# Dilated window attention in a three-layer kernel: scores in four accumulators, value transposes one projection later, and sums spread by products on all rows

## The chip, the core and the metric

The kernel runs on one core of a Trainium2 chip. Its engines work side by side, each in the order of its own queue: TensorE (PE; its weight loads are listed as PEld), VectorE (DVE), ScalarE (ACT), GpSimd (POOL) and SyncE (SP), which here only issues DMAs. The metric is the device time of the whole program in microseconds, as the median of several runs. All data are fp32.

## What is computed

Two layers of a first block (gated linear attention beside latent attention) and one layer of a second block (three dilated window attentions, a spatial gating unit, cross attention to a memory, and a feed-forward part). The change touches the dilated attention alone. For 512 tokens and three groups of four heads of width 64 it computes, cut down:

```python
for gi, (win, dil) in enumerate(((128, 1), (512, 4), (2048, 16))):
    # query t sees keys t, t-dil, ..., t-win
    s = q @ k.T * 64 ** -0.5 - slope * distance      # masked outside the window
    mx = max(s); e = exp(s - mx); den = sum(e)
    outs.append(e @ v / den); lses.append(mx + log(den))
alpha = softmax(stack(lses), axis=0)                  # over the three groups
y_attn = sum(alpha[..., None] * outs, axis=0)
```

## The kernel before

`mixer` is the second block's first stage. All its projections are matrix products in three parts: weights and activations are split into a high and a low fp32r part, and `mm3` (L202 to L204) adds high by high, high by low and low by high. A projection of 128 output columns is 24 such products on 512 token columns. Weights come in units through `Weights.ahead`: SyncE loads halves of a unit into one of three raw buffers (L90), ScalarE casts the high part (L93), VectorE subtracts for the low part (L94). One unit is fetched ahead of the one in use.

Accumulators lie in pools: two of kind `z` (projections), two `tr` (transposes), three `s`, one `o`. Who asks for a buffer waits until its last reader is done. The order in which each engine meets the work is that of the code, adjusted by a scheduler that moves an instruction up where it reckons that the one ahead would wait.

For each group g, the code projects q and k (four projections, j = 0 to 3), then v. The projections run on activations that are not yet normalised; `r_cols` (L319, L322, L216) turns the sum of squares, which GpSimd adds up, into r, one number for each token, and `r_bcast` (L331, L333) spreads r over all rows as R. `place` multiplies a finished projection by R on VectorE (L1024, L1027). In group 0 `r_cols` stands after the projection j = 0 and `r_bcast` after j = 1.

`scores(g, t, qk)` handles 128 queries (block t of four). Two heads lie in each 128 rows of q and k, so a product (L1038) uses 64 rows, and `par` says which half; each half has an accumulator of its own, of kind `s`. VectorE then scales and adds the bias (L1047) and takes the maximum over the keys (L1049). Group 0 sees 256 keys from its second block on, the dilated groups 128. Group 0 calls `scores` for its four blocks after its v; a dilated group calls it for two blocks after each of the two v projections. An fp32 product outside `mm3` is two instructions in the trace, a transpose (L211) one.

`turn_values` transposes the projected v of a dilated group by blocks into `tr` accumulators, and ScalarE copies them out (L1057).

`maxima` transposes the 12 x 4 maxima for each group to four rows by 512 tokens, joins them there by VectorE (L1268, L1270), and transposes the result back as bias of the exponentials. `turn` and `values` then run over eight parts, with the projections of the gating unit as filling (`fill()` issues half a projection at a time). The sums of the exponentials are in `den`.

`spread` transposes the sums to four rows, adds them (L1293, L1295), takes the reciprocal (L1296), spreads it by a product of four rows with `sel` (L1300) over the 64 rows of each head, and multiplies (L1302). The spatial gating that follows normalises by L1196 to L1199 and mixes by products at L1206.

Of the kernel before, what the change touches and what calls it, by code (L numbers as in the profile page):

```python
# [10 lines left out]
F32 = mybir.dt.float32  # L11
F32R = mybir.dt.float32r
I32 = mybir.dt.int32
AF = mybir.ActivationFunctionType
ALU = mybir.AluOpType
# [138 lines left out]
class K:  # L154
# [836 lines left out]
    def mixer(self, scope):  # L991
# [38 lines left out]
        def scores(g, t, qk):  # L1030
            wide = g == 0 and t > 0
            n = 256 if wide else P
            kc = slice((t - 1) * P, (t + 1) * P) if wide else tsl[t]
            pss = [self.psum("s", (P, 2, 256)) for _ in range(2)]
            for i in range(2):
                for par in range(2):
                    b = slice(64 * par, 64 * par + 64)
                    nc.tensor.matmul(pss[par][:, i, 0:n], qk[b, i, tsl[t]], qk[b, 2 + i, kc],  # L1038
                                     start=True, stop=True)
            for par in range(2):  # L1040
                if g == 0:
                    S = S1[t // 2][:, t % 2, par::2, 256 - n:256]
                    bias = tb1[:, par::2, 256 - n:256]
                else:
                    S = S23[g - 1][:, t, par::2, :]
                    bias = tb23[g - 1][:, par::2, :]
                nc.vector.scalar_tensor_tensor(S, pss[par][:, :, 0:n], 0.125, bias,  # L1047
                                               ALU.mult, ALU.add)
                nc.vector.tensor_reduce(mx[:, 4 * g + t, par::2], S, AX, ALU.max)  # L1049

# [7 lines left out]

        for g in range(3):
# [3 lines left out]
            for j in range(4):  # L1063
                unit, c = (uq, uk)[j // 2], j % 2
                zs.append(self.feat_proj(unit, slice(c * P, (c + 1) * P), rhs,
                                         kind="zzss"[j] if g == 0 else "z"))
                if r is None:
                    _, r = self.r_cols()
                elif R is None:
                    R = self.mxp.tile([P, T], F32, name="Rmix")  # L1070
                    self.r_bcast(r, R[:])
                if R is not None:
                    for z in zs:
                        place(qk[:, j + 1 - len(zs) + zs.index(z), :], z, g)
                    zs = []
# [3 lines left out]
            if g == 0:  # L1079
# [4 lines left out]
                for t in range(NT):  # L1084
                    scores(g, t, qk)
            else:
                vT = [self.t2(), self.t2()]
                for c in range(2):
                    z = self.feat_proj(uv, slice(c * P, (c + 1) * P), rhs)
                    place(vT[c][:], z, g)  # L1090
                    for t in (2 * c, 2 * c + 1):
                        scores(g, t, qk)
                for t in range(NT):
                    turn_values(g, t, vT)
# [6 lines left out]
        fill.add(self.tok_fill(T, lambda t, z: nc.scalar.mul(ysb[:, t, :], z[:], r[:, t:t + 1])))  # L1101
        self.maxima(mx, fill)
        nM = self.nM
        den = self.att.tile([P, 12, 4], F32, tag="den", name="den", bufs=1)
        sel = self.att.tile([4, 4, 64], F32, tag="sel", name="sel", bufs=1)
        nc.vector.tensor_copy(sel[:], self.ident[0:4, 0:4, None].to_broadcast([4, 4, 64]))
# [150 lines left out]
    def maxima(self, mx, fill):  # L1257
# [4 lines left out]
        for g in range(3):  # L1262
# [8 lines left out]
            if g:  # L1271
                fill()
# [9 lines left out]
    def spread(self, den, sel, oT, yh, yl, fill):  # L1282
# [3 lines left out]
        M = self.t2()  # L1286
        for g in range(2):
# [8 lines left out]
        nc.vector.reciprocal(M[0:4, :], M[0:4, :])  # L1296
        fill()
        for hp in range(2):
            ps = self.psum("s")
            nc.tensor.matmul(ps[:], sel[:, 2 * hp:2 * hp + 2, :].rearrange("p h d -> p (h d)"),  # L1300
                             M[0:4, :], start=True, stop=True)
# [339 lines left out]
```

## Time and profile before

| | |
|---|---|
| median of 3 runs | 1296.17 us (1295.49 to 1297.13) |
| profiled execution, its own time | 1299.38 us |
| its span | 1297.5 us |
| TensorE busy | 1273.4 us, 98% |
| VectorE, ScalarE, GpSimd busy | 700.2, 516.9, 205.4 us |
| mean DMA rate | 96 GB/s |

TensorE is busy nearly all the time, so a place matters by what it adds to TensorE's own sequence: a wait, a product, or a stretch at a lower clock. The duration shown for a product contains its way through the array, which overlaps the next product; what a product takes of TensorE is the distance from its start to the next one's. The part of the program that changes lies at about 487 to 677 us of the span.

### The profile page before, as it was taken

The numbers are of one execution on the slowest core, as the hardware profiler recorded it, in microseconds if no ns is written. First come the engines' busy times: TensorE is split into PE (matmuls) and PEld (weight loads), VectorE is DVE, ScalarE is ACT, GpSimd is POOL, SyncE is SP. The second block draws the span as 40 slices with busy tenths as digits, with TensorE's granted clock in tenths as the row PEclk, the third lists the DMA queues.
The fourth block names the chain that finished last, engine by engine and source line by source line (L and its number), as shares of the span: only waits on it lengthen the run. The fifth ranks groups of instructions, "written<-read, shape, count | busy, mean of one in ns | idle before, by whom it ended". The sixth has DMA issues, their size and how long they took to land. (4 is left out here: it accounts for less than half of the span.)

```text
span 1297.5 us, 16404 instructions
## 1 busy us (share of the span) xinstructions
PE 1273.4 (98%) x6220; PEld 1035.0 (80%) x6220; DVE 700.2 (54%) x1290; ACT 516.9 (40%) x1171; POOL 205.4 (16%) x213
## 2 busy tenths in 40 slices
PE   7999999999999999999999999999999999999997
PEld 6777778888777878777878887887888888888886
DVE  6775645467555453645366546546655543555532
ACT  6663434357334342214733334445433322233231
POOL 6441000234100120000001002200311100011110
PEclk9999999999999999999999999999999999999999
DMA  7132015413111475221112233233222223323311
GB/s 245 38 115 82 33 33 167 148 45 126 47 40 66 111 241 167 74 90 65 62 61 89 93 110 103 92 114 99 71 91 98 72 90 123 113 96 98 106 52 65
DMA packets 39647, 124.29 MB, mean 96 GB/s; under 512 B 4783, under 2 KB 5297, under 8 KB 39441
## 3 DMA queue, kind: packets, MB, share of 16 engines
q1 hardware_dynamic: 37584, 116.80, 27.7%
q0 software_dynamic: 1840, 6.41, 1.7%
q8 instruction: 49, 0.80, 0.3%
q14 instruction: 30, 0.24, 0.1%
q10 hardware_dynamic: 144, 0.03, 0.0%
HBM read 116.94 MB, written 6.29 MB: 95 GB/s over the span
## 5 line engine op out<-in xcount | busy, mean ns | idle before, releaser
L93 ACT CAST whi<-wraw 128x512 fp32r<-128x512 f32 (+4 forms) x420 | 226.8, 595 | 331.9 <-PE psz L203 228.2
L94 DVE TENSOR_TENSOR wlo<-wraw,whi 128x512 fp32r<-128x512 f32 (+4 forms) x420 | 298.0, 750 | 89.4 <-ACT whi L93 77.6
L202 PE MATMUL psz<-u,whi 128*128 128x512 f32 x640 | 251.8, 394 | 0.0
L203 PE MATMUL psz<-u,whi 128*128 128x512 f32 x640 | 250.3, 391 | 0.5 <-DVE u L302 0.5
L204 PE MATMUL psz<-u,wlo 128*128 128x512 f32 x640 | 250.1, 391 | 0.0
L202 PEld LDWEIGHTS psz<-u,whi 128*128 128x128 f32 x640 | 120.4, 188 | 26.2 <-ACT t L1229 0.8
L203 PEld LDWEIGHTS psz<-u,whi 128*128 128x128 f32 x640 | 120.5, 188 | 25.8 <-DVE u L302 0.9
L204 PEld LDWEIGHTS psz<-u,wlo 128*128 128x128 f32 x640 | 120.4, 188 | 25.2
L202 PE MATMUL psz<-whi,u 128*128 128x512 f32 (+1 forms) x320 | 128.3, 401 | 0.0
L202 PE MATMUL psz<-big,whi 128*128 128x512 f32 (+1 forms) x328 | 126.0, 384 | 1.5 <-DVE t L915 1.5
L203 PE MATMUL psz<-big,whi 128*128 128x512 f32 (+1 forms) x328 | 125.0, 381 | 1.6 <-DVE big L1243 1.6
L204 PE MATMUL psz<-big,wlo 128*128 128x512 f32 (+1 forms) x328 | 124.9, 381 | 0.0
L204 PE MATMUL psz<-whi,u 128*128 128x512 f32 (+1 forms) x320 | 123.6, 386 | 0.0
L203 PE MATMUL psz<-wlo,u 128*128 128x512 f32 (+1 forms) x320 | 123.5, 386 | 0.0
L216 POOL TENSOR_TENSOR sm<-sm,mhalf 128x4 f32<-128x4 f32 (+2 forms) x38 | 36.1, 951 | 343.0 <-DVE sm L1197 186.5
L308 POOL TENSOR_TENSOR t<-t,t 128x512 f32<-128x512 f32 x35 | 51.6, 1474 | 196.8 <-ACT t L307 167.7
L202 PEld LDWEIGHTS psz<-whi,u 128*128 128x128 f32 x320 | 60.6, 189 | 18.5 <-issue 7.9
L1424 POOL TENSOR_TENSOR t<-t,t 128x512 f32<-128x512 f32 x22 | 34.3, 1561 | 255.2 <-DVE t L1422 242.7
L202 PEld LDWEIGHTS psz<-big,whi 128*128 128x128 f32 x328 | 61.7, 188 | 14.3 <-DVE t L915 1.9
L203 PEld LDWEIGHTS psz<-big,whi 128*128 128x128 f32 x328 | 61.7, 188 | 14.1 <-DVE big L1243 2.0
L204 PEld LDWEIGHTS psz<-big,wlo 128*128 128x128 f32 x328 | 61.7, 188 | 12.1
L204 PEld LDWEIGHTS psz<-whi,u 128*128 128x128 f32 x320 | 60.7, 190 | 12.0 <-issue 0.3
(331 smaller groups left out, 1859.9 us busy)
## 6 DMA issues: line engine op xcount, KB each, us to landing
wraw<-wts SPq DMA_DIRECT2D x166, 512.0 KB, 4.0
wraw<-wts SPq DMA_DIRECT2D x16, 384.0 KB, 3.3
wraw<-wts SPq DMA_DIRECT2D x16, 352.0 KB, 3.0
x<-t SPq DMA_DIRECT2D x16, 256.0 KB, 3.5
wraw<-wts SPq DMA_DIRECT2D x6, 464.0 KB, 4.8
t<-xT SPq DMA_DIRECT2D x8, 256.0 KB, 4.2
t<-x SPq DMA_DIRECT2D x8, 256.0 KB, 4.5
x<-x SPq DMA_DIRECT2D x8, 256.0 KB, 3.7
```

The lines of the kernel that those rows point to most:

```text
L93: nc.scalar.copy(hi[:, c:d], raw[:, c - a:d - a])
L94: nc.vector.tensor_tensor(lo[:, c:d], raw[:, c - a:d - a], hi[:, c:d].bitcast(F32), ALU.subtract)
L202: mm(out, lhsT[0], rhs[0], start=start, stop=False)
L203: mm(out, lhsT[0], rhs[1], start=False, stop=False)
L204: mm(out, lhsT[1], rhs[0], start=False, stop=stop)
L216: self.nc.gpsimd.tensor_tensor(out, a, self.mhalf[:, 0:n], ALU.pow)
L308: nc.gpsimd.tensor_tensor(self.sq[:], self.sq[:], s[:], ALU.add)
L1424: nc.gpsimd.tensor_tensor(gt[:], gt[:], up[:], ALU.mult)
```

## The change

- `scores` takes a set of blocks. It uses up to four accumulators, three `s` and the `o`, each of which now holds two blocks of a dilated group, and issues all products of the set before the first operation on VectorE.
- Group 0 does blocks 0 and 1 after its second value projection, and blocks 2 and 3 after the first projection of group 1. A dilated group does all four blocks after its first v projection; its `turn_values` come after the first projection of the next group, for the last group after half a projection of the filling.
- `r_cols` and `r_bcast` each stand one projection later.
- `maxima` joins the two dilated groups by one VectorE operation ahead of the transposes, so that there are two groups to transpose instead of three.
- `spread` clears all 128 rows of M (on GpSimd), splits M into two fp32r parts, and multiplies each of them with a `sel` of 128 rows in fp32r.

```diff
-        def scores(g, t, qk):
-            wide = g == 0 and t > 0
-            n = 256 if wide else P
-            kc = slice((t - 1) * P, (t + 1) * P) if wide else tsl[t]
-            pss = [self.psum("s", (P, 2, 256)) for _ in range(2)]
-            for i in range(2):
+        def scores(g, ts, qk):
+
+
+            banks, parts = iter("ssso"), []
+            for t in ts[::1 if g == 0 else 2]:
+                wide = g == 0 and t > 0
+                n = 256 if wide else P
+                pss = [self.psum(next(banks), (P, 2, 2, P)) for _ in range(2)]
+                for tt in (t,) if g == 0 else (t, t + 1):
+                    kc = slice((t - 1) * P, (t + 1) * P) if wide else tsl[tt]
+                    for i in range(2):
+                        for par in range(2):
+                            b = slice(64 * par, 64 * par + 64)
+                            dst = pss[par][:, tt - t, i, :]
+                            if g == 0:
+                                dst = pss[par][:, i].rearrange("p a k -> p (a k)")[:, 0:n]
+                            nc.tensor.matmul(dst, qk[b, i, tsl[tt]], qk[b, 2 + i, kc],
+                                             start=True, stop=True)
                 for par in range(2):
-                    b = slice(64 * par, 64 * par + 64)
-                    nc.tensor.matmul(pss[par][:, i, 0:n], qk[b, i, tsl[t]], qk[b, 2 + i, kc],
-                                     start=True, stop=True)
-            for par in range(2):
...
+            for S, bias, ps, m in parts:
+                nc.vector.scalar_tensor_tensor(S, ps, 0.125, bias, ALU.mult, ALU.add)
+                nc.vector.tensor_reduce(m, S, AX, ALU.max)
...
+        later = []
+
+        def projected():
+            if later:
+                later.pop(0)()
 
         for g in range(3):
...
                 zs.append(self.feat_proj(unit, slice(c * P, (c + 1) * P), rhs,
                                          kind="zzss"[j] if g == 0 else "z"))
-                if r is None:
+                projected()
+                if g == 0 and j == 1:
                     _, r = self.r_cols()
-                elif R is None:
+                if g == 0 and j == 2:
                     R = self.mxp.tile([P, T], F32, name="Rmix")
                     self.r_bcast(r, R[:])
...
-                for t in range(NT):
-                    scores(g, t, qk)
+                    if t == 1:
+                        scores(g, (0, 1), qk)
+                later.append(lambda qk=qk: scores(0, (2, 3), qk))
             else:
                 vT = [self.t2(), self.t2()]
                 for c in range(2):
                     z = self.feat_proj(uv, slice(c * P, (c + 1) * P), rhs)
                     place(vT[c][:], z, g)
-                    for t in (2 * c, 2 * c + 1):
-                        scores(g, t, qk)
-                for t in range(NT):
-                    turn_values(g, t, vT)
+                    if c == 0:
+                        scores(g, range(NT), qk)
+
+                def turned(g=g, vT=vT):
+                    for t in range(NT):
+                        turn_values(g, t, vT)
+
+                later.append(turned)
...
+        fill()
+        projected()
         self.maxima(mx, fill)
         nM = self.nM
         den = self.att.tile([P, 12, 4], F32, tag="den", name="den", bufs=1)
-        sel = self.att.tile([4, 4, 64], F32, tag="sel", name="sel", bufs=1)
-        nc.vector.tensor_copy(sel[:], self.ident[0:4, 0:4, None].to_broadcast([4, 4, 64]))
+        sel = self.att.tile([P, 4, 64], F32R, tag="sel", name="sel", bufs=1)
+        nc.vector.tensor_copy(sel[:], self.ident[:, 0:4, None].to_broadcast([P, 4, 64]))
...
         M = self.t2()
-        for g in range(3):
+        nc.vector.tensor_tensor(mx[:, 4:8, :], mx[:, 4:8, :], mx[:, 8:12, :], ALU.max)
+        for g in range(2):
             ps = self.psum("s")
...
-            if g:
                 fill()
...
         M = self.t2()
+        nc.gpsimd.memset(M[:], 0.0)
         for g in range(2):
...
         nc.vector.reciprocal(M[0:4, :], M[0:4, :])
+        M2 = [self.t2(dt=F32R), self.t2(dt=F32R)]
+        self.split(M2[0][:], M2[1][:], M[:])
         fill()
         for hp in range(2):
             ps = self.psum("s")
-            nc.tensor.matmul(ps[:], sel[:, 2 * hp:2 * hp + 2, :].rearrange("p h d -> p (h d)"),
-                             M[0:4, :], start=True, stop=True)
+            heads = sel[:, 2 * hp:2 * hp + 2, :].rearrange("p h d -> p (h d)")
+            for i in range(2):
+                nc.tensor.matmul(ps[:], heads, M2[i][:], start=i == 0, stop=i == 1)
             nc.vector.tensor_tensor(oT[hp][:], oT[hp][:], ps[:], ALU.mult)
```

Three places, as the instructions stand on an engine. On TensorE, the second score block of group 1 (accumulators `pss_…`, projection of the next group `psz_5056`, value transposes `pstr_…`), before:

```order
L1038 MATMUL pss_4991<-big_4797 128x128
L1038 MATMUL pss_4992<-big_4797 128x128
L1038 MATMUL pss_5001<-big_4797 128x128 x2
L211 MATMUL pstr_5011<-c_119,t_789_4917 128x128
L211 MATMUL pstr_5011<-c_119,t_790_4918 128x128
L211 MATMUL pstr_5015<-c_119,t_789_4917 128x128
L211 MATMUL pstr_5015<-c_119,t_790_4918 128x128
L202 MATMUL psz_5056<-u_4189,whi_4902 128x512
L1038 MATMUL pss_5002<-big_4797 128x128 x2
L211 MATMUL pstr_5019<-c_119,t_789_4917 128x128
```

and, of the change, from the middle of the one block of that group:

```order
L1046 MATMUL pss_4945<-big_4777 128x128
L1046 MATMUL pss_4946<-big_4777 128x128
L1046 MATMUL pss_4955<-big_4777 128x128
L1046 MATMUL pso_4956<-big_4777 128x128
L1046 MATMUL pss_4955<-big_4777 128x128
```

The products now alternate between two accumulators up to the end of the block, the last two of them `pss_4955` and `pso_4956`, and the transposes have left.

On VectorE, the same group: before, each half of the scores between two evacuations (L1027) of v projections:

```order
L1047 SCALAR_TENSOR_TENSOR big_4458<-pss_4946,big_4447 128x2x128
L1049 TENSOR_REDUCE mx<-big_4458 128x2 x2
L1047 SCALAR_TENSOR_TENSOR big_4458<-pss_4955,big_4447 128x2x128
L1047 SCALAR_TENSOR_TENSOR big_4458<-pss_4956,big_4447 128x2x128
L1049 TENSOR_REDUCE mx<-big_4458 128x2 x2
L1027 TENSOR_TENSOR t_790_4918<-psz_4965,Rmix 128x512
L94 TENSOR_TENSOR wlo_5042<-wraw_0_5043,whi_5041 128x512
L1047 SCALAR_TENSOR_TENSOR big_4458<-pss_4991,big_4447 128x2x128
```

and now:

```order
L1027 TENSOR_TENSOR t_789_4917<-psz_4919,Rmix 128x512
L1060 SCALAR_TENSOR_TENSOR big_4458<-pss_4945,big_4447 128x2x128 x2
L1061 TENSOR_REDUCE mx<-big_4458 128x2 x2
L1060 SCALAR_TENSOR_TENSOR big_4458<-pss_4946,big_4447 128x2x128 x2
L1061 TENSOR_REDUCE mx<-big_4458 128x2 x2
L1060 SCALAR_TENSOR_TENSOR big_4458<-pss_4955,big_4447 128x2x128 x2
L1061 TENSOR_REDUCE mx<-big_4458 128x2 x2
L1060 SCALAR_TENSOR_TENSOR big_4458<-pso_4956,big_4447 128x2x128 x2
L1061 TENSOR_REDUCE mx<-big_4458 128x2 x2
L1027 TENSOR_TENSOR t_790_4918<-psz_4981,Rmix 128x512
L94 TENSOR_TENSOR wlo_5022<-wraw_0_5023,whi_5021 128x512 x2
L94 TENSOR_TENSOR wlo_5022<-wraw_1024_5029,whi_5021 128x512 x2
```

All sixteen operations stand in one piece, ahead of the second evacuation and of the split of the next weight unit.

On TensorE, where the sums are spread (`psz` are projection products of the filling), before:

```order
L204 MATMUL psz_5860<-u_4190,wlo_5546 128x512
L1300 MATMUL pss_5822<-t_878_5808,sel 128x512
L1300 MATMUL pss_5827<-t_878_5808,sel 128x512
L202 MATMUL psz_5900<-u_4189,whi_5545 128x512
L203 MATMUL psz_5900<-u_4191,whi_5545 128x512
```

and now, with `t_872` and `t_873` the two parts of the sums:

```order
L204 MATMUL psz_5854<-u_4190,wlo_5533 128x512
L1332 MATMUL pss_5814<-t_872_5810,sel 128x512
L1332 MATMUL pss_5820<-t_872_5810,sel 128x512
L202 MATMUL psz_5894<-u_4189,whi_5532 128x512
L1332 MATMUL pss_5814<-t_873_5811,sel 128x512
L1332 MATMUL pss_5820<-t_873_5811,sel 128x512
L203 MATMUL psz_5894<-u_4191,whi_5532 128x512
```

Two products have become four, with one projection product between the high and the low parts.

## Rows read from the trace of the kernel before

**Rows 1.** The page: the span, and TensorE's busy us, share and instructions.

```profile
span 1297.5 us, 16404 instructions
...
PE 1273.4 (98%) x6220; PEld 1035.0 (80%) x6220; DVE 700.2 (54%) x1290; ACT 516.9 (40%) x1171; POOL 205.4 (16%) x213
```

**Rows 2.** Waits of TensorE's weight loads, 440 to 700 us: total us, times, longest.

```profile
PEld pss L1038 <- DVE big L1047: 3.6, 7, 0.7
```

**Rows 3.** Timeline of TensorE, column sums: start us, us, line, operands, count.

```profile
487.76 0.40 PE L204 MATMUL psz<-u,wlo 128*128 128x512 f32 x1
488.56 1.05 PE L319 MATMUL pstr<-c,t 128*128 128x1 f32 x8 [0.40 <-POOL t L308]
```

**Rows 4.** The same timeline at group 0's scores, in order of time.

```profile
518.47 0.28 PE L204 MATMUL psz<-whi,u 128*128 128x256 f32 x1
...
519.90 1.13 PE L1038 MATMUL pss<-big 64*128 64x256 f32 x8
...
524.64 1.13 PE L1038 MATMUL pss<-big 64*128 64x256 f32 x4
...
526.28 0.40 PE L202 MATMUL psz<-u,whi 128*128 128x512 f32 x1
```

**Rows 5.** The same timeline at group 1's two score blocks.

```profile
551.91 0.39 PE L204 MATMUL psz<-u,wlo 128*128 128x512 f32 x1
552.23 0.71 PE L1038 MATMUL pss<-big 64*128 64x128 f32 x8
...
553.86 0.71 PE L1038 MATMUL pss<-big 64*128 64x128 f32 x4 [0.48 <-DVE big L1047]
554.50 0.50 PE L202 MATMUL psz<-u,whi 128*128 128x512 f32 x1
554.84 0.40 PE L203 MATMUL psz<-u,whi 128*128 128x512 f32 x1
...
559.85 0.39 PE L204 MATMUL psz<-u,wlo 128*128 128x512 f32 x1
...
563.73 0.39 PE L204 MATMUL psz<-u,wlo 128*128 128x512 f32 x1
```

**Rows 6.** The same timeline at group 2's second score block and the maxima.

```profile
598.23 0.39 PE L204 MATMUL psz<-u,wlo 128*128 128x512 f32 x1
...
602.98 0.39 PE L204 MATMUL psz<-u,wlo 128*128 128x512 f32 x1
...
605.28 0.60 PE L211 MATMUL pss<-c,mx 128*4 128x128 f32 x4
```

**Rows 7.** The same timeline where the sums are spread.

```profile
669.54 0.39 PE L204 MATMUL psz<-u,wlo 128*128 128x512 f32 x1
669.86 1.98 PE L1300 MATMUL pss<-t,sel 4*128 4x512 f32 x4
...
672.10 0.39 PE L203 MATMUL psz<-u,whi 128*128 128x512 f32 x1
```

**Rows 8.** Stretches: length, busy PE, PEld, DVE, ACT, POOL, granted clock, DMA share, GB/s.

```profile
669.00:673.00 4.00, 4.00 (x14) 2.14 (x13) 3.32 (x7) 1.35 (x3) 0.55 (x1) 1.00 0.01 3
673.00:677.00 4.00, 4.00 (x16) 3.30 (x14) 1.26 (x2) 1.24 (x3) 0.00 (x0) 0.57 0.00 0
```

**Rows 9.** Groups by line, 500 to 690 us: busy us, mean ns, idle before.

```profile
L94 DVE TENSOR_TENSOR wlo<-wraw,whi 128x512 fp32r<-128x512 f32 x48 | 30.5, 684 | 0.8 <-ACT whi L93 0.8
L1027 DVE TENSOR_TENSOR big<-psz,Rmix 128x512 f32<-128x512 f32 x8 | 8.6, 1070 | 24.2 <-PE psz L204 24.2
L1047 DVE SCALAR_TENSOR_TENSOR big<-pss,big 128x256 f32<-128x256 f32 x18 | 6.7, 412 | 9.1 <-PE pss L1038 9.1
L1296 DVE RECIPROCAL t<-t 4x512 f32<-4x512 f32 x1 | 3.3, 3333 | 0.0
L207 ACT CAST big<-t 128x512 fp32r<-128x512 f32 x2 | 1.2, 624 | 1.0 <-DVE t L1302 1.0
```

**Rows 10.** Line 1487, the one memset of GpSimd on 128x512: shortest/median/longest ns.

```profile
L1487 POOL MEMSET AT<- x1: 550/550/550, 11.0 to 11.0; 128x512 f32 x1
```

## What the change will do to the time

> **What bounds the kernel now.** I read the page first: TensorE is busy for 1273.4 of the span's 1297.5 us [rows 1], so time can only be won where TensorE waits, runs below its full clock, or issues products that the sum does not need. I then looked, in the waits of TensorE, for the stretch that the diff touches (from about 487 to 677 us of the span), and in the timeline for how each stop looks. The reader is to see four places.
>
> First, the score products of line 1038 stand out in the waits: their weight loads wait for the vector engine's L1047, which empties the accumulators [rows 2]. Second, the column sums (L319) stand 0.80 us after the product before them, and wait for GpSimd [rows 3]. Third, score products that go to two accumulators in turn start in pairs: eight last 0.71 us where four that go to one accumulator last the same 0.71 us, and with 256 columns eight last 1.13 us and so do four [rows 4, 5]. Fourth, after the four-row products of L1300 the granted clock falls to a mean of 0.57 from 673 to 677 us, while TensorE is busy without a break [rows 7, 8].
>
> A unit for all that follows: between 554.84 and 559.85 us lie 22 projection products [rows 5], 5.01/22 = 0.228 us each. What a place costs is its stretch on TensorE less 0.228 for each projection product in it.
>
> **The score blocks, before.** Group 1, first half: 551.91 to 554.84 holds two projection products, 2.93 - 0.46 = 2.47 us. Second half with half of the value transposes: 559.85 to 563.73 holds three, 3.88 - 0.68 = 3.20. Together 5.67 [rows 5]. Group 2's first half repeats the 2.47; its second half, with transposes and eight transposes of maxima, runs from 598.23 to 602.98 with three products, 4.75 - 0.68 = 4.07; four more transposes of maxima at 605.28 cost 0.11 each, 0.44 [rows 6]. Together 6.98. Group 0: 518.47 to 526.28 holds six products of 512 columns and one of 256 (half of 0.228, say 0.12), 7.81 - 1.37 - 0.12 = 6.32 [rows 4].
>
> **The score blocks, after.** Every block alternates its two accumulators and has four of them, so I take no wait and all products in pairs. A block's price comes from the four unpaired products of 553.86: 0.64 until the next product starts at 554.50, that one keeps the place for 0.34 instead of 0.23, and the way in cost 0.32 instead of 0.23 (551.91 to 552.23): 0.64 + 0.11 + 0.09 = 0.84 for four slots [rows 5], and 0.11 for each further slot. All scores of a dilated group are 32 instructions, 16 slots: 0.84 + 12 x 0.11 = 2.16. With the eight value transposes, which pass at 0.11 (as those of the maxima do), group 1 costs 2.16 + 0.88 = 3.04 and **gains 2.6**. Group 2 costs 3.04 plus eight transposes of maxima (four are gone, since the two dilated groups are joined by one small vector operation): 3.92, and **gains 3.1**. In group 0 a slot of 256 columns costs 0.105 more (1.13 against 0.71 for four). Its first block (four slots of 128, four of 256) costs 0.84 + 0.44 + 0.42 = 1.70, its second (eight of 256) 1.28 + 0.84 = 2.12; 3.82 against 6.32 **gains 2.5**.
>
> **What the moved pieces queue behind.** On VectorE all 16 operations of a group now stand in a row: 16 x 0.41 = 6.6 us [rows 9]. Behind them stand the evacuation of the next projection (1.07) and the four splits of a weight unit (4 x 0.68), done some 11.4 us after the block begins. The unit is first needed after the block and three projections, 2.2 + 3 x 5.5 = 18.6 us: covered by 7 us. In group 0's second block the first projection of group 1 waits behind eight operations of twice the size, 8 x 0.68 = 5.4, which start when the first four slots are through (1.1): done, with its own 1.07, at 7.6 us, and its accumulator is wanted at 2.1 + 5.5 = 7.6. There is no cover here, and I take 0. The value transposes have two accumulators, so the third waits for a copy by ScalarE; a cast of twice that size takes 0.62 [rows 9], so both groups together lose between 0 and 1.2, and I take 0.5, nearer to the half-size copies.
>
> **Column sums.** They now stand a projection later (5.5 us), and GpSimd's sum, on which they wait, is done by then: 0.80 - 0.23 = 0.57, less the normal way in, **gains 0.5** [rows 3]. The spread of r follows a projection after, as before. The rescaled projections wait a projection longer for R, under 5.5 us of products.
>
> **The spread.** From 669.54 to 672.10 with two projection products: 2.56 - 0.46 = 2.10 us for the two four-row products [rows 7]. They become four of one pass each, as the projections' are: 4 x 0.228 = 0.91, **gains 1.2**. Added ahead of them: a cast on ScalarE (0.62) and a subtraction on VectorE (about 0.68). They follow the reciprocal of 3.33 us [rows 9], which now starts some 0.7 earlier (an operation of 512 columns, as the splits are), since a normalisation no longer stands ahead of it. So the first part is ready about when L1300 started, and the low part is wanted three products (0.68) later: I take 0, at most 1.3 if neither is covered. The memset costs 0.55 on GpSimd [rows 10], which is busy for 16% of the span [rows 1], and the buffer that it clears was last read by the fifth of the eight parts of the values: 0. The wider copy of sel lies in the stage's first projection: 0.
>
> **The clock.** From 673 to 677 the mean clock is 0.57, its lower level (1.2 of 2.4 GHz) for most of it: 4 x 0.43 = 1.7 us lost [rows 8]. The four-row products right before are the only thing there that the rest of the stage lacks; they become products on all rows, so I count **1.7** as gained. The Trainium skill, TensorE: Matmul & The Clock Gate, Part 1, lays a fall of the clock to TensorE standing idle between products. By that rule these products are no cause, the fall stays, and the time would be 1286.8. Here the trace disagrees so far: TensorE is busy 4.00 of the 4.00 us before the fall.
>
> **The sum.** 2.5 + 2.6 + 3.1 + 0.5 + 1.2 + 1.7 - 0.5 = 11.1 us. The profiled execution (1299.38, span 1297.5) would become 1288.3; it lies 3.2 us above the median of the runs, 1296.17, from which I take the same: **1285.1**. By its own bounds (no new wait: 1284.6; 1.3 at the spread and 0.7 more at the transposes: 1287.1) this case reaches from 1283.8, with the spread of the runs before, to 1287.1.
>
> **Rivals.**
> The fall of the clock stays, because something else sets it off or because runs without a profile do not have it. For it: one fall in one profile is thin proof. Against it: the place. 1285.1 + 1.7 = 1286.8.
> New waits take part of it back: the accumulator of group 1's first projection (no cover), value transposes queued on ScalarE behind a whole unit's four casts (2.5 us), the low part of the sums. 3 us of it: 1288.1.
> The pairs do not form with the new mix of accumulators. Then a dilated group needs 32 slots, 16 x 0.11 = 1.8 more, twice, and group 0 some 2.9 more: 1291.6. Against it: the pairs of today also go to two accumulators.
> Nothing comes of it: the waits move on to other accumulators, 1296. For it: VectorE, not TensorE, empties them, and its work is the same.
> **Slower:** the bursts on VectorE delay the weights. The splits free the three raw buffers, so a late split also delays the next load. If the two bursts of 6.6 and the 5.4 of group 0 were exposed in full, 18.6 less 11.1 gives 1303.7. It decides when a split comes over 7 us later than I reckoned. Against it: the cover just worked out.
>
> **How the numbers follow.** A measurement of this kernel can tell about 0.2%, 2.6 us. Forecast 0.60, clock stays 0.17, new waits 0.11, no pairs 0.05, nothing 0.04, slower 0.03. The first four are faster by over 0.2%: 0.93; within 0.2%: 0.04; slower 0.03. The likeliest is 1285.1. From 1283.8 to 1288.6 the first three cases lie; they hold 0.88, less what falls beyond their ends.
>
> **What would show it.** Right: no wait of score products for VectorE, scores of a dilated group in one block of about 2.1 us with all in pairs, no gap ahead of L319, the four spread products in about 0.9 us, and a granted clock of 1.00 from there on. Wrong: projections that wait for an evacuation (L1027), for the casts or splits of weights, or spread products that wait for the sums' split; and a stretch at the lower clock anywhere in this stage.

## The result and the profile after

The changed kernel took **1286.56 us** (median of 5 runs, 1284.45 to 1287.96) against 1296.17 of the kernel before: a ratio of 0.9919, 95% interval 0.9899 to 0.9939. Run once more beside later experiments it took 1285.23 us (0.9918, 0.9900 to 0.9936). The profiled execution took 1287.96, its span 1286.2. The page of the changed kernel, beside [rows 1]:

```profile
span 1286.2 us, 16406 instructions
...
PE 1266.1 (98%) x6216; PEld 1032.9 (80%) x6216; DVE 696.8 (54%) x1291; ACT 518.4 (40%) x1172; POOL 206.1 (16%) x214
```

TensorE is busy 7.3 us less and its idle time shrinks from 24.1 to 20.1 us. Next the waits of its weight loads from 440 to 700 us (total us, times, longest), beside [rows 2]:

```profile
PEld pss L1046 <- issue: 1.1, 3, 0.4
...
PEld pstr L211 <- ACT va L1069: 0.5, 2, 0.3
...
PEld pss L1332 <- ACT t L207: 0.2, 1, 0.2
PEld pss L1332 <- DVE t L208: 0.2, 1, 0.2
```

The wait of score products for VectorE (3.6 us in seven places) is gone. What has come is small: value transposes wait for ScalarE's copies (0.5), and the spread products for the two parts of the sums (0.2 each).

The timeline of TensorE at the column sums, beside [rows 3] (start us, us, line, operands, count):

```profile
493.00 0.39 PE L204 MATMUL psz<-u,wlo 128*128 128x512 f32 x1
493.23 0.95 PE L319 MATMUL pstr<-c,t 128*128 128x1 f32 x8
...
494.36 0.40 PE L203 MATMUL pss<-u,whi 128*128 128x512 f32 x1
```

They start 0.23 us behind the product ahead of them, where it was 0.80. With the unit of the prediction (a stretch less 0.228 for each projection product in it, called *net* below) the place, with two projection products in it, costs 1.36 - 0.46 = 0.90. In the kernel before the stretch from 487.76 ends at

```profile
489.79 0.39 PE L203 MATMUL psz<-u,whi 128*128 128x512 f32 x1
```

which is 2.03 - 0.46 = 1.57.

The one block of all scores of group 1, beside [rows 5]:

```profile
548.39 0.39 PE L204 MATMUL psz<-u,wlo 128*128 128x512 f32 x1
548.71 1.27 PE L1046 MATMUL pss<-big 64*128 64x128 f32 x17
549.71 0.27 PE L1046 MATMUL pso<-big 64*128 64x128 f32 x1
...
550.70 0.50 PE L202 MATMUL psz<-u,whi 128*128 128x512 f32 x1
551.03 0.39 PE L203 MATMUL psz<-u,whi 128*128 128x512 f32 x1
```

From 548.39 to 551.03 lie two projection products: 2.64 - 0.46 = 2.18 net, without a stop inside, two instructions side by side to the end.

Where the sums are spread, and the first mixing product of the gating unit behind it, beside [rows 7]:

```profile
660.72 0.39 PE L204 MATMUL psz<-u,wlo 128*128 128x512 f32 x1
660.94 0.69 PE L1332 MATMUL pss<-t,sel 128*128 128x512 f32 x2
661.47 0.40 PE L202 MATMUL psz<-u,whi 128*128 128x512 f32 x1
661.71 0.65 PE L1332 MATMUL pss<-t,sel 128*128 128x512 f32 x2
662.19 0.39 PE L203 MATMUL psz<-u,whi 128*128 128x512 f32 x1
662.42 0.40 PE L204 MATMUL psz<-u,wlo 128*128 128x512 f32 x1
...
664.94 0.39 PE L203 MATMUL psz<-u,whi 128*128 128x512 f32 x1
665.58 1.13 PE L1233 MATMUL pss<-wsT,big 128*128 128x128 f32 x8 [0.25 <-DVE big L1226]
...
666.78 0.39 PE L202 MATMUL psz<-u,whi 128*128 128x512 f32 x1
```

The spread costs 660.72 to 662.42, three projection products: 1.70 - 0.68 = 1.02 net instead of 2.10. But the mixing product now waits for VectorE: 664.94 to 666.78, with two projection products, is 1.84 - 0.46 = 1.38 net, where the mixing products after it cost 0.89 each. Half a microsecond is given back here.

The clock in stretches of the changed kernel, beside [rows 8] (length, then busy PE, PEld, DVE, ACT, POOL, granted clock, DMA share, GB/s):

```profile
20.00:24.00 4.00, 2.12 (x11) 1.58 (x10) 4.00 (x5) 3.82 (x8) 2.09 (x2) 1.00 0.78 244
24.00:28.00 4.00, 4.00 (x13) 3.43 (x12) 4.00 (x7) 3.08 (x6) 2.43 (x1) 0.57 0.49 154
51.00:55.00 4.00, 4.00 (x16) 2.32 (x15) 3.10 (x9) 3.35 (x11) 2.88 (x5) 1.00 0.00 0
55.00:59.00 4.00, 4.00 (x11) 2.57 (x10) 1.51 (x4) 1.09 (x4) 3.97 (x8) 0.50 0.28 76
...
664.00:668.00 4.00, 3.75 (x21) 2.94 (x20) 2.89 (x6) 1.34 (x5) 1.20 (x2) 1.00 0.00 0
```

Behind the spread the clock stays at 1.00. It falls elsewhere: after a stretch in which TensorE was idle for nearly half (20 to 24 us), and at 55 us, after TensorE was busy 4.00 of 4.00. What stands just ahead of the second fall are products of the decay gates (L431), fp32 on 17 rows. The kernel before had a fall there too, in its second layer, from 281 us. Over the whole span the mean granted clock of this profiled execution is 0.995, and 0.996 in that of the kernel before: one fall is gone, but the others weigh more.

The whole stage can be measured from the column sums of the mixer to those of the cross attention (L319 to L319), which start here in the kernel before, then in the changed kernel:

```profile
836.77 0.50 PE L319 MATMUL pstr<-c,sqmem 128*128 128x1 f32 x4
```

```profile
825.73 0.50 PE L319 MATMUL pstr<-c,sqmem 128*128 128x1 f32 x4
```

From 488.56 the kernel before took 348.21 us, one projection of 5.45 included that now lies ahead, so 342.76; the changed kernel takes 332.50 from 493.23. With the 0.57 saved ahead of the first of them that is 10.8 us.

### The profile page after: what moved, and what is told of

The parts are those of the page before. It is cut to its first block, busy times and chain, and to the rows that moved or that the text cites. A ratio compares the mean times of both kernels' runs of the same rounds, so it can differ in the third digit from the quotient of the medians.

```text
span 1286.2 us, 16406 instructions
## 1 busy us (share of the span) xinstructions
PE 1266.1 (98%) x6216; PEld 1032.9 (80%) x6216; DVE 696.8 (54%) x1291; ACT 518.4 (40%) x1172; POOL 206.1 (16%) x214
## 5 line engine op out<-in xcount | busy, mean ns | idle before, releaser
L94 DVE TENSOR_TENSOR wlo<-wraw,whi 128x512 fp32r<-128x512 f32 (+4 forms) x420 | 297.2, 749 | 94.1 <-ACT whi L93 93.1
L203 PEld LDWEIGHTS psz<-wlo,u 128*128 128x128 f32 x320 | 60.7, 190 | 10.7 <-issue 1.0
```

The costliest lines, as they stand in the source:

```text
L94: nc.vector.tensor_tensor(lo[:, c:d], raw[:, c - a:d - a], hi[:, c:d].bitcast(F32), ALU.subtract)
L203: mm(out, lhsT[0], rhs[1], start=False, stop=False)
```

## The experiments

All times are medians. The runs were made in four batches, each with runs of the kernel before beside them (medians 1296.03, 1296.03, 1296.89 and 1296.27); the ratios and intervals are to these. Places are compared by their net cost on TensorE, and whole stages by the distance L319 to L319 (332.50 in the changed kernel), since a median of the same program moved by 1.3 us from batch to batch. Each place and distance is read from one profiled execution. Some edits move the line numbers by one.

**The old spread.** The changed kernel with the four-row spread of before:

```diff
-        sel = self.att.tile([P, 4, 64], F32R, tag="sel", name="sel", bufs=1)
+        sel = self.att.tile([4, 4, 64], F32, tag="sel", name="sel", bufs=1)
...
-        M2 = [self.t2(dt=F32R), self.t2(dt=F32R)]
-        self.split(M2[0][:], M2[1][:], M[:])
...
-            for i in range(2):
-                nc.tensor.matmul(ps[:], heads, M2[i][:], start=i == 0, stop=i == 1)
+            nc.tensor.matmul(ps[:], sel[:, 2 * hp:2 * hp + 2, :].rearrange("p h d -> p (h d)"),
+                             M[0:4, :], start=True, stop=True)
```

> The changed kernel with the old spread alone: one four-row fp32 product for each pair of heads, no split of the sums. Theory: the stretch of the spread goes back from about 0.9 to 2.1 us, and in some of the runs, by chance of where they fall, the granted clock drops right behind these products (1.7 us): median 1287.7 to 1289.4. Rival (the drop of the clock seen there before had nothing to do with the four-row products): the 1.2 us alone, 1287.7, and never a drop at this place.

Measured: 1286.86 us (ratio 0.9921, 0.9905 to 0.9936), distance 333.12. The spread costs 2.11 again, but the first mixing product 0.90, so the new spread is worth 0.6 in place of 1.2, and no fall stood behind the four-row products in this profile. The median is below both forecasts, which had left out what the next stage gives back. Why the mixing product is late in the changed kernel is in the timeline of ScalarE, changed kernel first:

```profile
660.24 0.62 ACT L207 CAST t<-t 128x512 fp32r<-128x512 f32 x1 [4.94 <-DVE t L1324]
660.76 0.63 ACT L1223 ACTIVATE t<-big 128x512 f32<-128x512 f32 x1
```

and the kernel with the old spread:

```profile
653.67 0.64 ACT L1223 ACTIVATE t<-big 128x512 f32<-128x512 f32 x1
```

The cast of the sums' high part makes ScalarE wait 4.94 us for the reciprocal (L1324), and the squares (L1223) with which the gating unit's normalisation begins are queued behind it. Without that cast they run 7 us earlier on the clock of the profile, of which 1.4 is that this kernel reaches the spread that much sooner.

**The old scores.** The changed kernel with the score blocks, their places and the value transposes of before (two accumulators for each block of 128 queries, `scores` called for one block at a time):

```diff
...
-                    if t == 1:
-                        scores(g, (0, 1), qk)
-                later.append(lambda qk=qk: scores(0, (2, 3), qk))
+                for t in range(NT):
+                    scores(g, t, qk)
...
-                    if c == 0:
-                        scores(g, range(NT), qk)
+                    for t in (2 * c, 2 * c + 1):
+                        scores(g, t, qk)
+                for t in range(NT):
+                    turn_values(g, t, vT)
```

> The changed kernel with the old score blocks, the old places of their calls and of the value transposes; column sums, maxima and spread stay as changed. Theory: the score products wait for VectorE again (3.6 us of weight loads), the dilated blocks lose half of their pairs, and the three terms of the sum come back without the four transposes of maxima: 2.5 + 2.6 + 2.6 - 0.5 = 7.2 us, 1293.8. Rival (the blocks only moved the waits elsewhere): under 3 us, below 1289.5.

Measured: 1292.01 us (0.9964, 0.9950 to 0.9978), distance 339.82, which is 7.3 more, as the theory had it (7.2). The score blocks are the greater part of the gain.

**The products by accumulator.** The same blocks and places, with all products of one accumulator queued before those of the other, no alternation:

```diff
-                for tt in (t,) if g == 0 else (t, t + 1):
-                    kc = slice((t - 1) * P, (t + 1) * P) if wide else tsl[tt]
-                    for i in range(2):
-                        for par in range(2):
+                for par in range(2):
+                    for tt in (t,) if g == 0 else (t, t + 1):
+                        kc = slice((t - 1) * P, (t + 1) * P) if wide else tsl[tt]
+                        for i in range(2):
```

> The changed kernel with the products of a score block ordered by accumulator: all of one half of the rows, then all of the other, instead of in turn. Places, accumulators and VectorE's work as changed. Theory (half of the gain at the scores is the pairs): a dilated group takes 32 slots of 0.11 instead of 16, 1.8 us more, twice, and group 0 some 2.9 more: 6.5 us, 1293. Rival (the gain is only the missing wait, and a few more slots are hidden): within 1.5 us of 1286.6.

Measured: 1287.72 us (0.9929, 0.9914 to 0.9944), distance 334.25. The rival held. The same block of group 1 in this kernel's timeline:

```profile
546.37 0.39 PE L204 MATMUL psz<-u,wlo 128*128 128x512 f32 x1
546.68 1.93 PE L1046 MATMUL pss<-big 64*128 64x128 f32 x21
548.35 0.37 PE L1046 MATMUL pso<-big 64*128 64x128 f32 x1
548.45 0.27 PE L1046 MATMUL pss<-big 64*128 64x128 f32 x1
...
549.43 0.50 PE L202 MATMUL psz<-u,whi 128*128 128x512 f32 x1
549.77 0.40 PE L203 MATMUL psz<-u,whi 128*128 128x512 f32 x1
```

In the code all products of the last `pss` stand ahead of those of `pso`, yet the last of the one and the first of the other start in turn: products on one half of the rows begin while those on the other half still run. Whether the engine or the scheduler brought them together isn't shown, since the trace has their starts and not the order of the queue. The block costs 3.40 - 0.46 = 2.94, which is 0.76 more. At 0.11 a slot that is 7 slots lost of the 16 that full pairing saves. Alternating matters, but by 1.75 us in all and not by the 6.5 of the rival in the prediction.

**The gates on all rows.** The lower clock behind L431 suggested an edit outside the change. The 17 rows of gate weights stand in a tile of 128, cleared elsewhere, and the product takes all 128 rows (the memset that follows in the code now sets all 128 rows of `lrT` to ones, so the added rows hold ones, times zero):

```diff
-        self.wgu = self.lay.tile([LR + 1, 256], F32, name=f"wgu{l}", tag="wgu")
-        self.nc.gpsimd.dma_start(self.wgu[:], self.I["wgu"][l])
+        self.wgu = self.lay.tile([P, 256], F32, name=f"wgu{l}", tag="wgu")
+        self.nc.gpsimd.memset(self.wgu[:], 0.0)
+        self.nc.gpsimd.dma_start(self.wgu[0:LR + 1, :], self.I["wgu"][l])
...
-        L.lrT = self.t2([LR + 1, T])
+        L.lrT = self.t2([P, T])
```

> The changed kernel, with the forget gate's products of both layers of the first block (L431, 17 rows) on 128 rows, the added rows of the weights cleared. Not a part of the change: the same idea at the two places where few-row products are left. Both drops of the clock that the profiles of before and after show inside the first block, at 281 and at 55 us, begin behind these products. Theory (products on few rows set the drops off, by chance of where they fall): no drop behind L431 in any run, mean clock 0.997 to 0.998 in nearly all of them, median 1284.5 to 1285.6. Rival (the drops are chance and have another cause): runs as those of the changed kernel, 1286.6 and clocks from 0.995.

Measured: 1283.46 us (0.9893, 0.9873 to 0.9914); no fall behind the gates in the profile. This is below both forecasts; more on it further down.

**The spread five times over, on four rows and on all rows.** These two tell whether few rows have to do with the clock. The first has the old spread, each product issued five times; the second the same fp32 products on 128 rows, of which 124 are cleared:

```diff
...
-            for i in range(2):
-                nc.tensor.matmul(ps[:], heads, M2[i][:], start=i == 0, stop=i == 1)
+            for _ in range(5):
+                nc.tensor.matmul(ps[:], sel[:, 2 * hp:2 * hp + 2, :].rearrange("p h d -> p (h d)"),
+                                 M[:], start=True, stop=True)
```

(with `M[0:4, :]` in the four-row kernel).

> The changed kernel with the spread of the sums as it was before (fp32, four rows of weights), and each of its two products issued five times over, which adds work that the result does not need. One such product took 2 x 0.59 us in the trace of the kernel with the old spread, and its stretch 2.11 us for two, so ten take about 10.6 to 11.8 us, where the changed spread takes 1.04 and gives 0.5 back behind it: +9.1 to +10.3 us at full clock. Theory (products on four rows are what the clock falls behind): the granted clock reads 0.5 inside or behind the ten products, and the time is 1297.5 to 1301. Rival (falls come at random, whatever the rows): no fall there, 1295.5 to 1297.

> The same five-fold fp32 products, but on all 128 rows, of which 124 hold cleared values: the same count of columns and the same TensorE time as the four-row kernel of this call, +9.1 to +10.3 us on 1286.56. Theory (few rows are what the clock falls behind): the granted clock stays at 1.0 through and behind them, 1295.5 to 1297, some 2 to 4 us less than the four-row kernel. Rival (falls have nothing to do with rows): the same time as the four-row kernel within 1 us.

Measured: 1299.22 us on four rows (1.0030, 1.0016 to 1.0044), 1291.71 on all rows (0.9963, 0.9952 to 0.9974): 7.5 us between them. The mean granted clock is 0.990 to 0.993 in the ten runs on four rows, and 0.996 to 0.999 in the nine on all rows. The stretches on four rows:

```profile
657.70:662.00 4.30, 4.30 (x11) 1.96 (x11) 1.50 (x3) 0.72 (x1) 0.55 (x1) 0.99 0.00 0
662.00:668.00 6.00, 6.00 (x8) 2.30 (x7) 1.38 (x2) 0.62 (x1) 0.00 (x0) 0.50 0.00 0
668.00:674.00 6.00, 6.00 (x11) 3.03 (x10) 1.38 (x2) 1.24 (x3) 0.00 (x0) 0.50 0.00 0
```

and on all rows:

```profile
662.00:668.00 6.00, 6.00 (x17) 2.99 (x16) 2.06 (x3) 0.62 (x1) 0.00 (x0) 1.00 0.00 0
668.00:674.00 6.00, 6.00 (x34) 5.14 (x34) 3.29 (x7) 2.38 (x5) 0.99 (x1) 1.00 0.00 0
```

TensorE is busy without a break in both. On four rows the clock is at its lower level from 662 us on, four microseconds after the products begin, and still through the projection products behind them, up to 674; on all rows it does not move. The theory on rows holds. The distances, 346.53 and 339.66, lie 6.87 apart, which is what some 13.7 us at half the clock cost (estimated from the stretches, 661.9 to 675.5): the clock is the whole difference.

The time of the second was lower than expected, though: its 20 instructions cost 8.62 net, 0.43 each, where I had reckoned with the 0.53 (2.11/4) of those on four rows. That figure was wrong for these too: on four rows the products start 0.43 apart as well while the clock is full, and 0.85 at the lower level; the 0.53 had spread about 0.4 us for the ends of the block over four instructions. So it is luck that the four-row time lies in its forecast: the products cost less than reckoned, and the fall more.

**Four accumulators at the old places.** The new blocks, called where the old ones were (two blocks of 128 queries at a time in the dilated groups, value transposes at the group's end):

```diff
...
-                    if c == 0:
-                        scores(g, range(NT), qk)
-
-                def turned(g=g, vT=vT):
-                    for t in range(NT):
-                        turn_values(g, t, vT)
-
-                later.append(turned)
+                    scores(g, (2 * c, 2 * c + 1), qk, ("ss", "so")[c])
+                for t in range(NT):
+                    turn_values(g, t, vT)
```

> The changed kernel's alternation of four accumulators, but with the blocks of scores, and the value transposes, issued at the places of the kernel before (dilated groups: two slots at a time, each behind its own half of the mask work, transposes of values at the group's end). The old blocks at the old places cost +7.3 us in the trace between the two column-sum products. Theory (the wait for the query and key copies ahead of each block is most of that, and moves away only with the place): +4 to +5.5 us of the 7.3 are back, 1290.5 to 1292. Rival (the accumulators are most of it, the place little): +1 to +3 us, 1287.5 to 1289.5.

Measured: 1288.48 us (0.9940, 0.9924 to 0.9956), distance 335.45. Of the 7.3 us of the scores 4.4 come with the new blocks and their accumulators, 2.95 with the place; the rival held. Half of the latter is in group 0, whose two blocks now meet without a projection between them:

```profile
518.17 0.70 PE L1046 MATMUL pss<-big 64*128 64x256 f32 x2 [0.72 <-DVE big L1060]
```

**Column sums, spread of r and maxima as before.**

```diff
-                if g == 0 and j == 1:
+                if r is None:
                     _, r = self.r_cols()
-                if g == 0 and j == 2:
+                elif R is None:
...
-        nc.vector.tensor_tensor(mx[:, 4:8, :], mx[:, 4:8, :], mx[:, 8:12, :], ALU.max)
-        for g in range(2):
+        for g in range(3):
```

> The changed kernel with the column sums of the mixer and their spread a projection earlier, as before, and with the maxima turned in three groups instead of two joined ones. The column-sum product had 0.91 us net of its projection in the changed kernel and 1.57 before, the spread of the roots 0.90 and 1.13, and the turns of one group of maxima are 0.44 to 0.51. Theory (each of these is on the path, none is given back): +1.2 to +1.5 us, 1287.8 to 1288.1. Rival (they are caught by other waits): within 0.4 us of 1286.56.

Measured: 1289.27 us (0.9945, 0.9928 to 0.9961), 2.7 above the changed kernel, more than either theory said. The trace has 1.8 of it: the column sums cost 1.19 net (0.91 in the changed kernel), the turned values and maxima 2.44 (2.00), and the spread of r 1.98 (0.90):

```profile
493.30 1.16 PE L331 MATMUL pss<-c,sm 128*128 128x128 f32 x8 [0.82 <-POOL sm L216]
```

It waits for GpSimd's roots, which the prediction had passed over ("follows a projection after, as before"). The kernel before has this wait in one of its two profiles: with the gates' edit alone (below) the spread of r costs 2.44 there, against 1.13 in the profile of the prediction, and the column sums 0.90:

```profile
492.13 1.16 PE L332 MATMUL pss<-c,sm 128*128 128x128 f32 x8 [1.28 <-POOL sm L216]
```

The roots are late because L322, from which they follow, is queued on VectorE behind a split (L94) that waits for ScalarE's cast (6.14 us idle here, 5.92 there). In the changed kernel that split is done before the sums are there, and VectorE waits 0.39 us for them. The rest of the 2.7 is within what a median moves between batches.

**The gates again, beside the changed kernel, and on the kernel before.** The first is the changed kernel itself, the second the edit of the gates on it, the third that edit alone on the kernel before.

> The changed kernel itself once more, beside the two below, so that they are compared in one call. Both theories expect its time again, 1285.5 to 1287.5.

> The changed kernel with the products of the decay gates on all 128 rows, once more (their 17 rows of weights stand in a tile whose other rows are cleared). Theory (products on few rows are what the clock falls behind, and few are left then): 1.5 to 4 us below the changed kernel of this call. Rival (the first time was a draw of the falls that vary from run to run): within 1 us of it.

> The kernel before with this edit of the gates alone, and nothing of the change; its spread of the sums stays on four rows. Theory (the edit is worth the same wherever it is made, since the gates lie ahead of the changed stage): 1.5 to 4 us below the 1296.03 of before, and the granted clock 1.0 behind the gates' products of both layers. Rival (the falls only move to the next place on few rows, the spread): within 1 us of 1296.03, with the clock at 0.5 behind the spread.

Measured: 1285.23, 1283.61 (0.9894, 0.9881 to 0.9908) and 1293.50 us (0.9975, 0.9962 to 0.9988). By the medians the edit is worth 1.6 in this batch and 3.4 on the kernel before. Against the first median of the changed kernel, which is of another batch, it was 3.1; the ratios of this batch, 0.9918 and 0.9894, also lie 3.1 us apart. The six runs of the changed kernel in it reach from 1284.62 to 1291.19, so their median leaves room for both. Its profile on the kernel before keeps 1.00 behind the gates and falls behind the four-row spread:

```profile
284.00:288.00 4.00, 4.00 (x23) 3.45 (x22) 2.36 (x5) 3.28 (x12) 1.91 (x5) 1.00 0.00 0
...
668.00:672.00 4.00, 4.00 (x12) 2.57 (x11) 3.24 (x5) 2.31 (x5) 0.38 (x1) 0.69 0.00 0
```

The same stretch of the gates in the changed kernel of this batch:

```profile
284.00:288.00 4.00, 4.00 (x10) 2.75 (x9) 1.54 (x5) 2.53 (x5) 3.54 (x6) 0.51 0.00 0
```

Not all of it is the clock. In a profile without falls at the gates (the one with products by accumulator) the timeline has

```profile
51.10 0.34 PE L204 MATMUL pss<-whi,big 128*128 128x384 f32 x1
...
55.57 0.40 PE L202 MATMUL psz<-whi,u 128*128 128x512 f32 x1
```

and with the gates on all rows, for the same products,

```profile
50.72 0.34 PE L204 MATMUL pss<-whi,big 128*128 128x384 f32 x1
...
54.26 0.39 PE L202 MATMUL psz<-whi,u 128*128 128x512 f32 x1
```

Between the two rows of each lie eight instructions of the gates and the same six projection products: 4.47 against 3.54 us, 0.93 less at full clock. The same reading in the second layer (277.22 to 281.46, and 275.85 to 278.97) gives 4.24 against 3.12, 1.12 less. So 2.05 us of the gain have nothing to do with the falls, and the medians can't tell how much is left for them.

**The cast on VectorE.** The gates on all rows, and the high part of the sums cast by VectorE, so that ScalarE's queue is free:

```diff
-        self.split(M2[0][:], M2[1][:], M[:])
+        nc.vector.tensor_copy(M2[0][:], M[:])
+        nc.vector.tensor_tensor(M2[1][:], M[:], M2[0][:].bitcast(F32), ALU.subtract)
```

> The kernel with the gates on all rows, and the cast of the sums' high part on VectorE instead of ScalarE. In the changed kernel ScalarE stood idle for 4.94 us at that cast, waiting for the reciprocal, with the first block's normalisation (L1223) queued behind it, and the first mixing product then cost 1.39 us net of its projection products, against 0.90 in the kernel with the old spread, where the same normalisation ran ahead of the reciprocal. Theory (the queue behind the cast is what gives 0.5 us back): the normalisation runs ahead of the reciprocal, the first mixing product costs 0.90, the four spread products still about 1.0, and the whole is 0.5 us lower, 1282.9 to 1283.1, which the median can hardly tell from 1283.5; the trace decides. Rival (the longer queue of VectorE holds back the spread products or the mixing operand): 1.3 us or more for the spread, or 1.3 or more at the first mixing product, and 1283.5 to 1284.2.

Measured: **1281.48 us** (1281.10 to 1284.13; ratio 0.9893, 0.9875 to 0.9910), distance 331.95. ScalarE, then the first mixing product on TensorE:

```profile
648.69 0.63 ACT L1224 ACTIVATE t<-big 128x512 f32<-128x512 f32 x1
```

```profile
657.94 0.39 PE L204 MATMUL psz<-u,wlo 128*128 128x512 f32 x1
658.17 1.05 PE L1234 MATMUL pss<-wsT,big 128*128 128x128 f32 x8
...
659.29 0.40 PE L203 MATMUL psz<-u,whi 128*128 128x512 f32 x1
```

The squares run ahead of the reciprocal, the mixing product costs 1.35 - 0.46 = 0.89, and the spread still about 1.0: the half microsecond is back. With the gates' edit alone the mixing product costs 1.39 and the distance is 332.41, so it is the cast that does it. Of the medians, this is the lowest of the study; how far it lies below the kernel without this last edit (1283.46 and 1283.61) the runs can't tell, since they weren't made in one batch.

## Why the prediction held, and where its terms were off

The forecast of 1285.1 (1283.8 to 1288.6) held with 1286.56 and 1285.23. By its steps:

- **Score blocks: right, to a tenth.** Forecast 2.16 net for a dilated group; 2.18 in both. Group 0: 1.70 and 2.12 forecast, 1.70 and 2.13 measured. The value transposes cost 0.95 in group 1 (0.88 without a wait) and with the maxima 2.00 in group 2 (1.76), so 0.3 of the 0.5 set aside for waits on ScalarE came. 2.5 + 2.6 + 3.1 - 0.5 = 7.7 was forecast; measured 6.32 - 3.83 = 2.5, 5.67 - 3.14 = 2.5 and 6.98 - 4.19 = 2.8, together 7.8. Put back at the old form and place they cost 7.3.
- **No cover at group 1's first projection, and the bursts on VectorE: right.** No wait for an evacuation (L1027) or a split (L94) is among the waits of the changed stage; the slower rival did not come.
- **Column sums: mis-sized, 0.5 forecast, 0.9 measured.** 0.67 at the sums themselves and 0.23 at the spread of r, which [rows 3] does not reach and the prediction put at nothing. The experiment that undid it cost 1.4 at the two places, and against the second profile of the kernel before the gain is 1.5, all of it at the spread of r.
- **The spread: mis-sized, 1.2 forecast, 0.6 measured.** Four products do cost 1.0 and not 2.1; the waits for the two parts, 0.2 each, are inside this 1.0, which was forecast as 0.9. The step that failed is "added ahead of them: a cast on ScalarE". I asked when its result would be ready, and not what is queued behind it while it waits. The list of new waits named ScalarE at another place. The queue held back the next stage by 0.5 us, and the cast on VectorE shows that it was the cause.
- **The clock: right in direction, not shown at its size.** The fall behind the spread is in three of the four profiles with four-row products (not in that of the old spread) and in none of the ten on all rows. With five times the products the granted clock of all ten runs shows it, and it costs 6.9 us. So the rival by the Trainium skill, "TensorE: Matmul & The Clock Gate", Part 1, which lays a fall to an idle TensorE, does not hold here: TensorE was busy without a break ahead of it. It does agree with the fall at 24 us, behind 2.12 busy of 4.00. But a fall comes in some executions only, and 1.7 is its price where it comes; undoing the spread moved the median by 0.3 and 1.6 us against the two medians of the changed kernel, the 0.6 of the path included. What I counted in full belongs to one execution.
- **The pairs: the price of that rival was wrong.** Without alternation 1.75 us are lost, not 6.5, since products on the two halves of the rows still overlap. Whether the two halves or the two accumulators make a pair the runs don't show: each half has an accumulator of its own.

With the measured terms the sum is 7.8 + 0.9 + 0.6 + 1.7 = 11.0 us for the two profiles, against 11.1 forecast: the two mis-sized terms nearly cancelled each other, which is luck. The distances show 10.8. The medians moved by 9.6 and by 11.7; that they lie on both sides of a forecast that holds the whole fall of one execution is in part luck too.

## What to carry to other kernels

When an operation is added to an engine that has time to spare, look at what is queued behind it for as long as it waits: a cast of 0.6 us kept the first step of the next stage waiting behind it for 4.94. In the kernel before the split ahead of L322 could do the same on VectorE. A block of products on few rows cost more than the same block on 128 rows, 0.3 to 0.4 us for each block of the gates at full clock, though in the spread the products themselves start 0.43 us apart on 4 rows as on 128; behind some of these blocks the clock falls as well. Operands that fill 128 rows, the added ones of the weights cleared, gave 1.6 to 3.4 us in this kernel. A term that rests on an event of one profiled execution should be weighed by how often executions show it.

## What was unexpected of the hardware

The granted clock fell to 1.2 GHz while TensorE was busy without a break, behind fp32 products on 17 rows (six of ten profiles; none of four with these products on 128 rows) and on 4 rows (three of four, one of them with five times the products; none of ten). Four profiles without a fall at the gates are few; what rests on more is the pair of kernels with five times the products. In the four-row kernel it stayed down from 662 to 674 us and longer, as long as they went on and a little beyond. Two instructions on different halves of the rows start side by side, even where the code has eight of one kind ahead of those of the other.

Two things stay open. A fall near 130 us is in four of the profiles. Ahead of it stand, in all four, products of the linear attention on 64 rows (L593, L643) and on 128, and one wait of 0.3 us, with TensorE busy for 4.7 of the 5 us before; other profiles have the same products and no fall, and no run undid them. Nor do the runs say why the falls behind few rows come in one execution and not in the next.
